# Hybrid encoder step on one core: the outputs of key and value rows issued from ScalarE instead of SyncE

## The chip, the cores and the metric

The kernel runs on one core of one Trainium2 chip. The time is that of the device for one execution, in microseconds (us), and the median of several runs counts. The profile is a recording of one further execution. Its engines are PE (TensorE; PEld is the load of its weights, beside PE), DVE (VectorE), ACT (ScalarE), POOL (GpSimd) and SP (SyncE), which here does nothing but issue transfers (DMAs) and wait. SPq is SP's time in issuing.

## The reference

One layer of an encoder is computed for 1024 prompt rows and 64 sample rows (1088 in all, width 1024), the samples with 512 cached rows before them. Cut to what matters here:

```python
u = rms_norm(h)
z = split_cols(u @ W_in)           # one projection: columns of A, B and C
A = rwkv7_mixer(z['a_*'])          # delta rule with a matrix state, 8 heads
B = fox_attention(b_q, b_k, b_v)   # 8 heads of 64, with a forget gate
C = dsa_attention(c_q, c_k, c_v)   # indexer, top-k of keys, 2 key/value heads
h = h + concat[A*silu(g_A), B*silu(g_B), C*silu(g_C)] @ W_out
# returned beside y: p_b_k, p_b_v, p_c_k, p_c_v (1024 rows each)
#                and s_b_k, s_b_v, s_c_k, s_c_v (64 rows each)
```

So every key and value row is an output as well as an operand of the attention.

## The kernel before, in words

The columns of `W_in` are loaded in blocks of 128 (`load_w`: the block `wraw` is loaded from SP at L130, ACT, POOL split it into three parts `wh`, `wl`, `wb`), and `proj` (L154) multiplies each by the whole of `u`: these matmuls, named `pproj`, are 1088 in each of three kinds. A block's result is "parked": written to a buffer in device memory, from where the attention loads it later. The blocks are projected by generators which yield after every few matmuls, and which the program pumps between the steps of dependent work (top-k, the RWKV units of A, the first attention), so that PE finds projection work while a chain of small steps runs. The order of instructions on each engine is set before the run by a scheduler, from the program's order and a model of its own; each engine then runs its list strictly in order.

The keys of a block are parked by `park_keys`, the values by `park_values`; there are four blocks of two heads for B (`b_k0` to `b_k3`, `b_v0` to `b_v3`) and one for C (`c_k0`, `c_v0`). Both call `rows_out`, ten calls in all. It turns the block (columns by rows) with PE in nine squares, ACT copies these in three steps from PSUM to a tile `rows` of 128 x 9 x 128 (L730), and two DMAs write it to the outputs: L731 the 1024 prompt rows (512 KB), L732 the 64 sample rows (32 KB). In `park_values` the tile is then split into high and low halves by ACT (L771) and POOL (L774), for each of the two heads (`vs` for the new rows, `vcs` for the cached ones), and written to `b_v..` (L775).

Three things tie other work to these two DMAs:

- `rows`, `vs`, `vcs`, `kT`, `kh`, `zg` and others are all tiles of one ring, tag "z", of `NZ=4` buffers. In one call of `park_values` six are taken: `vT`, `rows`, `vs`, `vcs`, `vs`, `vcs`. The sixth, the second `vcs`, gets the buffer of `rows`, so ACT's cast into it (L771) has to wait until both DMAs have read `rows` and landed.
- Every DMA of the kernel is issued from SP, in one order: loads of the attention's operands (`fetch`, L865: `K`, `KL`, `Q`, `QS`, `VS`; gates `sg`, L1117), of weights (L130), stores of parked data. A DMA whose operand isn't there holds those behind it.
- Completions are counted on eight semaphores in turn (DMAHW0 to DMAHW7), over the issues of all engines: each DMA waits until the DMA eight issues earlier has landed.

The attention of B (FoX) runs from about 741 us on: per step, PE computes scores (`ps_sc`, L974 and L975), DVE adds and takes the maximum (L917), ACT the exponential (L921), PE turns the result (`ps_atp`, L107), ACT and DVE split it (`hl`, L943, L944), PE multiplies with the values (`ps_pv`, L1005). That of C follows, and the output projection (L1726) is pumped into it from about 1043 us.

Of the kernel before, what the change touches and what calls it, by code (L numbers as in the profile page):

```python
# [24 lines left out]
P = 128  # L25
# [60 lines left out]
class K:  # L86
# [632 lines left out]
    def rows_out(self, xT, out_p, out_s):  # L719

        nc = self.nc
        row = self.z("rows").rearrange("p (a d) -> p a d", d=P)
        for g in range(3):
            ps = self.tp()
            nb = 4 if g < 2 else 1
            r = P if g < 2 else 64
            for j in range(nb):
                i = 4 * g + j
                self.turn(ps[:r, j * P:(j + 1) * P], xT[:, i * P:i * P + r])
            nc.scalar.copy(row[:r, 4 * g:4 * g + nb, :], ps[:r, :nb * P].rearrange("p (a d) -> p a d", a=nb))  # L730
        nc.sync.dma_start(out=out_p.rearrange("(a p) d -> p a d", p=P), in_=row[:, 0:8, :])  # L731
        nc.sync.dma_start(out=out_s, in_=row[:64, 8, :])  # L732
        return row

    def park_keys(self, col, name, cache, out_p, out_s):
# [1210 lines left out]
```

## Time and profile before

| | before |
|---|---|
| runs | 1293.16, 1289.9, 1292.87 us |
| median | 1292.87 us |
| profiled execution, time | 1289.49 us |
| its span on the core | 1286.6 us |
| PE busy | 1230.5 us (96%) |
| ACT busy | 780.3 us (61%) |
| DVE busy | 843.0 us (66%) |
| POOL busy | 671.7 us (52%) |
| mean granted clock of PE | 0.991 |

The span is from the first to the last instruction of the core. The execution's own time is 2.9 us above it. PE is busy nearly all the time, so what counts is where it isn't: the profile gives each engine's busy time in any stretch, what ended each idle time, and the share of its full speed that PE's clock was granted there.

### The profile page before, as it was taken

The page shows a single profiled execution, that of the slowest core. Times are in us where ns is not written, and L with a number is a line of the kernel's source. Part 1 is how long each engine was busy: PE and PEld are TensorE (multiplying, and loading weights), DVE is VectorE, ACT ScalarE, POOL GpSimd, SP SyncE. Part 2 cuts the span into 40 slices and gives each one's busy share as a digit, 9 for nine tenths or more (in the row PEclk, how much of TensorE's full clock was granted, in tenths as well). Part 3 has the DMA queues.
Part 4 walks back from the last instruction along what each step waited for, and adds up shares of the span by engine and source line. Part 5 has one row for each costly group of instructions (what it writes and reads, how often), then busy time and mean ns, then how long its engine had stood idle before and what let it go on. Part 6 is the DMA issues. An engine that isn't in the chain of part 4 may idle for free.

```text
span 1286.6 us, 29362 instructions
## 1 busy us (share of the span) xinstructions
PE 1230.5 (96%) x10563; PEld 941.8 (73%) x10563; DVE 843.0 (66%) x2487; ACT 780.3 (61%) x1762; POOL 671.7 (52%) x973
## 2 busy tenths in 40 slices
PE   7999999999999999988999989999999889999997
PEld 5777777777777777666777767888887756777764
DVE  7468458888887787998564136556665588666642
ACT  7345357788877888544344456676664587655531
POOL 6333444545545655646454555576666477444311
PEclk9999999999999999989999999999999999999999
DMA  8332421232332443325225389676756476534323
GB/s 231 108 104 68 138 85 52 68 100 71 90 96 73 125 132 105 116 83 170 90 73 162 115 233 268 191 217 201 200 155 183 130 217 171 146 104 114 87 82 95
DMA packets 171699, 168.77 MB, mean 131 GB/s; under 512 B 38641, under 2 KB 146209, under 8 KB 171426
## 3 DMA queue, kind: packets, MB, share of 16 engines
q1 hardware_dynamic: 171554, 166.91, 44.7%
q8 instruction: 83, 1.36, 0.4%
q14 instruction: 62, 0.51, 0.1%
HBM read 106.18 MB, written 62.25 MB: 131 GB/s over the span
## 4 chain that ended last, share of the span: by engine, by line
PE 78%; DVE 9%; DMA 6%; ACT 3%; issue 2%; SPq 1%; POOL 0%; DVEq 0%; POOLq 0%; ACTq 0%
PE pproj L154 37%; PE pproj L1726 7%; PE ps_pv L1005 5%; PE ps_atp L107 4%; PE ps_tp L1726 4%; PE ps_sc L974 2%; PE ps_sc L975 2%; PE ps_gb L1500 2%; PE ps_tp L107 1%; PE ps_gb L1507 1%; ACT junka L613 1%; PE ps_gc L1610 1%; PE ps_gc L1612 1%; PE ps_gc L1601 1%; PE ps_ga L107 1%
## 5 line engine op out<-in xcount | busy, mean ns | idle before, releaser
L154 PE MATMUL pproj<-uH,wh 128*128 128x384 f32 (+4 forms) x1088 | 491.4, 452 | 0.0
L154 PE MATMUL pproj<-uH,wl 128*128 128x384 f32 (+4 forms) x1088 | 361.6, 332 | 0.0
L154 PE MATMUL pproj<-uL,wb 128*128 128x384 bf16 (+4 forms) x1088 | 356.9, 328 | 0.8 <-DVE shift L818 0.5
L154 PEld LDWEIGHTS pproj<-uH,wh 128*128 128x128 f32 (+1 forms) x1088 | 215.8, 198 | 4.8 <-issue 0.7
L154 PEld LDWEIGHTS pproj<-uH,wl 128*128 128x128 f32 (+1 forms) x1088 | 206.5, 190 | 2.0
L154 PEld LDWEIGHTS <-wb 128*128 128x128 bf16 (+1 forms) x1088 | 105.8, 97 | 116.5 <-issue 80.5
L613 ACT ACTIVATE junka<-score,tk_tau 128x1024 f16<-128x1024 f32 (+4 forms) x160 | 149.5, 934 | 33.1 <-DVE junk L607 22.1
L926 POOL TENSOR_SCALAR S<-S,mx 128x128 f32<-128x128 f32 (+8 forms) x136 | 105.6, 780 | 84.1 <-DVE mx L925 62.6
L140 POOL TENSOR_TENSOR wl<-wraw,wh 128x256 fp32r<-128x256 f32 (+1 forms) x184 | 137.8, 780 | 5.8 <-ACT wh L137 4.8
L943 ACT CAST hl<-ps_atp 128x512 fp32r<-128x512 f32 (+3 forms) x184 | 93.6, 515 | 76.8 <-PE ps_atp L107 67.1
L944 DVE TENSOR_TENSOR hl<-ps_atp,hl 128x512 fp32r<-128x512 f32 (+3 forms) x184 | 109.7, 600 | 45.1 <-ACT hl L943 43.4
L921 ACT ACTIVATE S<-S,mx 128x128 f32<-128x128 f32 (+8 forms) x136 | 105.8, 778 | 39.6 <-DVE mx L917 36.1
L142 POOL TENSOR_SCALAR wb<-wraw 128x512 bf16<-128x512 f32 (+1 forms) x92 | 62.9, 701 | 114.3 <-PE pproj L154 66.9
L1005 PE MATMUL ps_pv<-hl,VS 128*128 128x256 f32 (+3 forms) x640 | 111.9, 286 | 7.6 <-ACT hl L943 3.4
L1005 PEld LDWEIGHTS ps_pv<-hl,VS 128*128 128x128 f32 (+1 forms) x640 | 88.7, 173 | 20.7 <-DVE hl L944 4.7
L107 PE MATMUL ps_atp<-ident,S 128*128 128x128 f32 x616 | 101.7, 276 | 1.1 <-DVE hl L944 0.6
L1171 POOL TENSOR_TENSOR cb<-nm,T 128x256 f32<-128x256 bf16 (+2 forms) x80 | 54.3, 685 | 54.5 <-DVE mx L917 52.7
L107 PEld LDWEIGHTS ps_atp<-ident,S 128*128 128x128 f32 x616 | 74.8, 141 | 7.8 <-issue 1.0
L137 ACT CAST wh<-wraw 128x1024 fp32r<-128x1024 f32 (+1 forms) x46 | 47.7, 1037 | 35.9 <-PE pproj L154 35.4
L1726 PE MATMUL pproj<-oh,gh 128*128 128x512 f32 x144 | 67.4, 490 | 0.8 <-ACT oh L1705 0.5
L1726 PE MATMUL pproj<-ol,gb 128*128 128x512 bf16 (+1 forms) x144 | 52.4, 386 | 0.9 <-DVE ol L1706 0.9
L1598 DVE COPY UV<-ps_gd 64x64 f32<-64x64 f32 x136 | 29.9, 220 | 28.7 <-PE ps_gd L1593 26.5
(387 smaller groups left out, 2845.2 us busy)
## 6 DMA issues: line engine op xcount, KB each, us to landing
wraw<-in_w_in_dram SPq DMA_DIRECT2D x45, 512.0 KB
oraw<-in_w_out_dram SPq DMA_DIRECT2D x12, 512.0 KB
out_dram<-rows SPq DMA_DIRECT2D x10, 512.0 KB
x<-in_x_prompt_dram SPq DMA_DIRECT2D x8, 512.0 KB
wt<-a_wa SPq DMA_DIRECT2D x16, 256.0 KB
b_v<-vs SPq DMA_DIRECT2D x8, 512.0 KB
VS<-b_v SPq DMA_DIRECT2D x8, 512.0 KB
d_y<-y SPq DMA_DIRECT2D x64, 64.0 KB
```

The lines of the kernel that those rows point to most:

```text
L107: self.nc.tensor.transpose(out, x, self.ident[:n, :n])
L140: nc.gpsimd.tensor_tensor(l[:, k:k + 2, :n], raw[:, k:k + 2, :n], h[:, k:k + 2, :n], op=OP.subtract)
L142: nc.gpsimd.tensor_scalar(b[:, k:k + 4, :n], raw[:, k:k + 4, :n], 1.0, 0.0, op0=OP.mult, op1=OP.add)
L154: self.nc.tensor.matmul(ps[:n, :nt], a[:, k, :n], b[:, k, t0:t0 + nt], start=(k == 0 and i == 0), stop=(k == KD - 1 and i == 2))
L613: nc.scalar.activation(junk[:, :sc.shape[1]], sc, AF.Sign, bias=tf[:, j:j + 1], accum_out=cnt[:, j:j + 1])
L921: nc.scalar.activation(S[:, :kn], S[:, :kn], AF.Exp, bias=mx[:, nm - 1:nm], scale=-1.0, accum_out=mx[:, 6:7])
L926: nc.gpsimd.tensor_scalar(S[:, :kn], S[:, :kn], mx[:, 7:8], 0.5, op0=OP.mult, op1=OP.mult)
L943: nc.scalar.copy(ph[:kr, a:b], ps[:kr, a:b])
L944: nc.vector.tensor_tensor(pl[:kr, a:b], ps[:kr, a:b], ph[:kr, a:b], op=OP.subtract)
L1005: nc.tensor.matmul(pv[0:m, q0:256], VS[:, kb, 0:m], hl[:, x, o:o + w], start=kb == 0 and x == 0, stop=at[-1][0] == last and n == 3)
L1171: nc.gpsimd.tensor_tensor(o, x, y, op=OP.add)
L1726: nc.tensor.matmul(ps[hf][:n, :], parts[m // 4][q][:, m % 4, :n], self.wo[m][q // 2][:, hf * 512:hf * 512 + 512], start=m == 0 and q == 0, ...
```

## The change

Both output DMAs of `rows_out` are issued by ACT (`nc.scalar`) instead of SP (`nc.sync`). ACT has written the rows. What is copied, to where, and the ring of buffers stay as they are.

```diff
             nc.scalar.copy(row[:r, 4 * g:4 * g + nb, :], ps[:r, :nb * P].rearrange("p (a d) -> p a d", a=nb))
-        nc.sync.dma_start(out=out_p.rearrange("(a p) d -> p a d", p=P), in_=row[:, 0:8, :])
-        nc.sync.dma_start(out=out_s, in_=row[:64, 8, :])
+
+        nc.scalar.dma_start(out=out_p.rearrange("(a p) d -> p a d", p=P), in_=row[:, 0:8, :])
+        nc.scalar.dma_start(out=out_s, in_=row[:64, 8, :])
         return row
```

Lines below it are one higher in the changed kernel (L731 becomes L732, L865 becomes L866). Twenty issues go from SP's list (804 rows before, 784 now) to ACT's. The scheduler sets the order of the other instructions anew as well: the lists are alike up to about 422 us, then differ in pieces, on every engine.

The first place is `b_v3`, the last block of values of B. On SP, before, the two issues stand behind the loads for the first two heads and for the sample queries (the last of these is the gate `sg` at L1117). In brackets is what an instruction waits for.

```order
L865 DMA QS_12081<-b_q0h 64x64 [waits DMAHW4_49]
L865 DMA QS_12082<-b_q0h 64x64 [waits DMAHW5_49,Pool_49]
L865 DMA QS_12082<-b_q0l 64x64 [waits DMAHW6_49]
L865 DMA QS_12082<-b_q0h 64x64 [waits DMAHW7_49]
L1117 DMA sg<-b_g_9844 128x1024 [waits DMAHW0_49]
L731 DMA out_dram<-rows 128x8x128 [waits DMAHW1_49]
L732 DMA out_dram<-rows 64x128 [waits DMAHW2_49]
L865 DMA K<-b_k0h 64x576 [waits DMAHW3_49,PE_49]
```

Now the loads of `K` follow directly on `sg` there. On ACT, in the changed kernel, the same two issues stand among the copies and casts of the rows (L730, L772) and the exponentials (L922):

```order
L922 ACTIVATE S,mx<-S,mx 128x128 [waits DVE_49]
L732 DMA out_dram<-rows 128x8x128 [waits DMAHW2_49,Activation_49]
L922 ACTIVATE S,mx<-S,mx 128x256 [waits DVE_49]
L772 CAST vs<-rows 128x8x64 [waits DMAHW7_49,Pool_49]
L772 CAST vcs<-kc 128x4x64 [waits DMAHW1_49]
L730 COPY rows<-ps_tp 64x128 [waits PE_49]
L772 CAST vs<-rows 128x8x64
L922 ACTIVATE S,mx<-S,mx 128x384 [waits DVE_49]
L733 DMA out_dram<-rows 64x128 [waits DMAHW6_49,Activation_49]
```

The cast into the buffer of `rows` comes seven rows later on ACT, behind the exponential of 640 keys; before the change it stood behind that of 1024 keys, three exponentials later:

```order
L922 ACTIVATE S,mx<-S,mx 128x640 [waits DVE_49]
L954 COPY tmp<-ps_pv 64x256 [waits PE_49]
L772 CAST vcs<-kc 128x4x64 [waits DMAHW6_49,DMAHW2_49,Pool_49]
L922 ACTIVATE S,mx<-S,mx 128x768 [waits DVE_49]
L944 CAST hl<-ps_atp 128x512 [waits PE_49]
```

So the cast waits for the two DMAs (their counters are DMAHW2 and DMAHW6) and for POOL, and it does so earlier in ACT's list than before.

The second place is SP about 25 us later, ahead of the first load of the next block's keys, `K<-b_k1h`. Before:

```order
L746 DMA c_k0h<-kcs 128x512 [waits DMAHW2_49,Activation_49]
L747 DMA c_k0l<-kcs 128x512 [waits DMAHW3_49,DVE_49]
L130 DMA wraw<-in_w_in_dram 128x8x128 [waits DMAHW4_49,Pool_49]
L865 DMA K<-b_k1h 64x1024 [waits DMAHW5_49,PE_49]
L865 DMA K<-b_k1h 64x1024 [waits DMAHW6_49]
```

In the changed kernel:

```order
L763 DMA kc<-in_cache_c_v_dram 128x4x128 [waits DMAHW0_49,PE_49]
L797 DMA b_g_12354<-zg 128x1088 [waits DMAHW1_49,DVE_49]
L747 DMA c_k0h<-kcs 128x512 [waits DMAHW2_49,Activation_49]
L866 DMA K<-b_k1h 64x1024 [waits DMAHW3_49,PE_49]
L866 DMA K<-b_k1h 64x1024 [waits DMAHW4_49]
```

The store `c_k0l` and the load of a block of weights, which stood ahead of it, now come behind it.

The third place is PE before the first matmul of the output projection. Between a run of six transposes (the same in both) and that matmul, the list before held 40 matmuls of the attention of C, whose last rows were:

```order
L975 MATMUL ps_sc<-KL,cQ 128x384
L1005 MATMUL ps_pv<-hl,VS 128x128
L1005 MATMUL ps_pv<-hl,VS 64x128
L1005 MATMUL ps_pv<-hl,VS 64x256
L1005 MATMUL ps_pv<-hl,VS 128x256
L107 MATMUL ps_atp<-ident,S 128x128 x3
L1726 MATMUL pproj<-oh_15961,gh 128x512 x2
```

In the changed kernel it holds 59, and ends so:

```order
L107 MATMUL ps_atp<-ident,S 128x128 x3
L975 MATMUL ps_sc<-K,cQ 128x512
L976 MATMUL ps_sc<-KL,cQ 128x512
L1006 MATMUL ps_pv<-hl,VS 128x128
L975 MATMUL ps_sc<-K,cQ 128x384
L976 MATMUL ps_sc<-KL,cQ 128x384
L1006 MATMUL ps_pv<-hl,VS 64x128
L1006 MATMUL ps_pv<-hl,VS 64x256
L1006 MATMUL ps_pv<-hl,VS 128x256
L107 MATMUL ps_atp<-ident,S 128x128 x3
L1727 MATMUL pproj<-oh_15961,gh 128x512 x2
```

Two pairs of scores, eight products with the values and seven transposes have moved ahead of the output projection's first matmul.

## Rows read from the trace of the kernel before

**Rows 1.** The page: busy us of each engine, share of the span, instructions.

```profile
PE 1230.5 (96%) x10563; PEld 941.8 (73%) x10563; DVE 843.0 (66%) x2487; ACT 780.3 (61%) x1762; POOL 671.7 (52%) x973
```

**Rows 2.** Windows: us busy of 20 by engine, PE's clock, DMA share, GB/s.

```profile
540.00:560.00 20.00, 14.82 (x147) 11.12 (x147) 18.65 (x40) 7.15 (x15) 13.01 (x17) 0.86 0.36 120
740.00:760.00 20.00, 18.99 (x119) 14.80 (x118) 5.42 (x23) 9.62 (x25) 13.64 (x25) 1.00 0.97 248
760.00:780.00 20.00, 15.45 (x92) 12.12 (x91) 12.17 (x39) 12.17 (x30) 7.42 (x11) 0.91 0.87 246
1020.00:1040.00 20.00, 13.11 (x79) 10.62 (x77) 15.57 (x57) 14.31 (x37) 12.13 (x21) 0.91 0.74 214
```

**Rows 3.** Everything on the tile rows: ns min/median/max, and who waited.

```profile
L730 ACT COPY rows<-ps_tp x30: 243/580/593, 418.7 to 845.0; 128x512 f32<-128x512 f32 x20, 64x128 f32<-64x128 f32 x10
...
L731 SPq DMA_DIRECT2D out_dram<-rows x10: 378/389/533, 421.4 to 840.9; - x10
L732 SPq DMA_DIRECT2D out_dram<-rows x10: 476/490/583, 423.6 to 846.0; - x10
...
  ACT vcs L771: 4.7, 2
```

**Rows 4.** Timeline of ACT, 744 to 776 us: start, duration, operation, idle before.

```profile
753.90 0.26 ACT L730 COPY rows<-ps_tp 64x128 f32<-64x128 f32 x1 [0.24 <-PE ps_tp L107]
...
758.64 0.37 ACT L953 COPY tmp<-ps_pv 64x256 f32<-64x256 f32 x1
...
766.34 0.19 ACT L921 ACTIVATION_READ_ACCUMULATOR S<-S,mx 128x1 f32 x1
770.17 0.40 ACT L771 CAST vcs<-kc 128x256 fp32r<-128x256 f32 x1 [3.65 <-DMA out_dram<-rows]
```

**Rows 5.** Timeline of SP's issues, 744 to 804 us.

```profile
764.28 0.43 SPq L731 DMA_DIRECT2D out_dram<-rows  x1
764.76 0.58 SPq L732 DMA_DIRECT2D out_dram<-rows  x1
...
788.67 0.44 SPq L747 DMA_DIRECT2D c_k0l<-kcs  x1
789.20 0.47 SPq L130 DMA_DIRECT2D wraw<-in_w_in_dram  x1
790.81 1.09 SPq L865 DMA_DIRECT2D K<-b_k1h  x2
```

**Rows 6.** The chain that ended last, 744 to 776 us: start, duration, what.

```profile
746.35 7.55 DMA sg<-b_g
...
753.91 8.56 DMA VS<-b_v
...
764.76 5.32 DMA out_dram<-rows
```

**Rows 7.** Timeline of PE, single rows at 771 and 797 us.

```profile
771.39 0.33 PE L1005 MATMUL ps_pv<-hl,VS 128*128 128x128 f32 x1 [3.41 <-ACT hl L943]
...
797.77 0.30 PE L974 MATMUL ps_sc<-K,Q 128*128 128x128 f32 x1 [0.52 <-DMA K<-b_k1h]
```

**Rows 8.** Windows of 2 us behind the stop (columns as in Rows 2).

```profile
768.00:770.00 2.00, 0.00 (x0) 0.00 (x0) 0.00 (x0) 0.00 (x0) 0.00 (x0) 1.00 1.14 355
770.00:772.00 2.00, 0.34 (x2) 0.21 (x2) 0.79 (x3) 1.83 (x7) 1.35 (x2) 1.00 1.06 230
772.00:774.00 2.00, 1.91 (x11) 1.35 (x11) 0.77 (x4) 1.53 (x5) 2.00 (x5) 0.72 1.06 233
774.00:776.00 2.00, 1.86 (x8) 1.56 (x9) 1.18 (x2) 0.46 (x1) 0.53 (x1) 0.50 1.01 227
776.00:778.00 2.00, 1.55 (x11) 1.27 (x10) 0.89 (x3) 1.23 (x3) 0.00 (x0) 0.93 0.99 370
```

**Rows 9.** Windows of 10 and 20 us around the output projection's start (columns as before).

```profile
1034.00:1044.00 10.00, 6.57 (x42) 5.12 (x42) 8.87 (x27) 8.16 (x19) 5.74 (x9) 1.00 0.71 203
1040.00:1060.00 20.00, 18.92 (x100) 11.69 (x101) 18.34 (x53) 17.16 (x38) 15.40 (x16) 1.00 0.69 195
```

## The prediction

> **What bounds the kernel.** I read the page first: PE is busy 96% of the span [rows 1], so a change can only win where PE stands, or lose by making it stand. The windows show where that is [rows 2]: most lose little, but 540 to 560 us has 14.82 of 20 us, 760 to 780 has 15.45 and 1020 to 1040 has 13.11. Of these only the second is near one of the ten places where rows are written out.
>
> I then asked for all that touches the tile `rows`, and for who waits on it [rows 3]. The issues take SP 389 and 490 ns in the median, ten times each, from 421 to 846 us. Only one wait on them is of any size: ACT's cast `vcs`, 4.7 us in two places. One of the two is the stop in the second stretch: ACT ends an exponential's sum at 766.34 + 0.19 = 766.53 us and stands for 3.65 us, until 770.17, for the output of `rows` to land [rows 4]; the other has the rest, 1.05 us. PE's product with the values then waits for ACT's `hl`, 3.41 us [rows 7], and the windows around it show every engine at nothing from 768 to 770 us [rows 8].
>
> Why it lands so late: the last copy of these rows starts on ACT at 753.90 us [rows 4], but SP issues the two outputs only at 764.28 and 764.76 [rows 5]. SP was not waiting for the rows. The chain shows what it waited for: the landing of `sg` (7.55 us) and of `VS` (8.56 us), loads of the attention that hold one of the eight completion counters each [rows 6]. From the last issue, the landing took 5.32 us [rows 6].
>
> **The change, part by part.**
>
> *The stop at 766 us, gain.* On ACT the first issue comes after the second copy of rows, at about 752 us, the second after the third copy, at about 755.5 us: some 12 and 9 us earlier. The counters they need were last held, by the new lists, by the first load of `Q`, four issues ahead of `sg`, and by `sg` itself, which landed at 746.35 + 7.55 = 753.90 [rows 6], so ACT should not stand there. Landing: at best 5.32 us after the issue, as the same output did under less load, at worst 8.56 us, as a load of 512 KB did in this very stretch, where the DMA share is 0.97 [rows 2, 6]. For the first output this gives 757 to 760.9 us, for the second (32 KB, behind it) 761 to 764. The cast now comes earlier in ACT's list, behind `tmp` that ends at 758.64 + 0.37 = 759.0 us [rows 4]. So it stands from nothing to 5 us there; PE was busy 18.99 of 20 us from 740 to 760 [rows 2], with projection work among its steps, which hides a stand of ACT of a microsecond or so; I take it at nothing, and its far end is rival 2. If the stop at 766 us is gone, PE gains its 3.41 us and the clock that it lost: the three windows behind it were granted 0.72, 0.50 and 0.93 of full speed [rows 8], a loss of (0.28 + 0.50 + 0.07) x 2 = 1.70 us. Together 5.11 us, the upper bound. The lower bound is 0.
>
> *How much of it stays.* PE's next wait for SP is at 797.77 us, 0.52 us for `K<-b_k1h` [rows 7], and from 764 us on the DMAs are at a share of 0.99 to 1.14 [rows 8]. SP comes free for this load at 789.20 + 0.47 = 789.67 us and issues it at 790.81, when PE has released the buffer [rows 5]. In the new order the rows' issues (0.43 + 0.58 us), the store of `c_k0l` (0.44) and a load of weights (0.47) no longer stand before it: SP can be free 1.92 us earlier, some 0.1 us of gaps more, at about 787.6 us. So the load can follow PE by 790.81 - 787.6 = 3.2 us, and what PE gains beyond that it stands for again at this load. I take 3.2 us as the gain.
>
> *ACT's new work, loss.* The issues cost ACT 10 x (0.389 + 0.490) = 8.8 us if they take as long there as on SP [rows 3]; the trace has no DMA issued by ACT. ACT is at 61% [rows 1], and in most of the stretch PE has projection work between ACT's steps. Lower bound 0; upper bound 8.8, if all of it lay on the path. Nearer is the first, since only `b_v3` lies among dependent steps, where two issues take 0.88 us; I take 0.5 us.
>
> *The other nine places.* The one other wait on `rows` is ACT's 1.05 us, and no row has PE standing behind it; what it could give is 0 to 1.05 us, and I take 0.
>
> *The new order, loss or gain.* At the output projection's start, 19 more matmuls of the attention come ahead of the first of the projection. In 1034 to 1044 us, where the last of the 40 ran, PE was busy 6.57 of 10 us [rows 9]. 19 matmuls at a mean of 6.57/42 = 0.156 us are 3.0 us of work and at that share another 1.5 us of standing. Later fewer such steps are left between projection work, but PE has only 1.08 us of standing in 1040 to 1060 to give back [rows 9]. Bounds: -1.1 (that is given back and the rest costs nothing) and +3.0 (an estimate: twice 1.5, since single large ones take 0.30 to 0.33 us [rows 7] and not 0.156); I take 1.3, near the middle. In 540 to 560 us DVE is busy 18.65 of 20 [rows 2] and its list there, the end of the top-k, is shuffled: bounds -2 and +2 (an estimate: two fifths of the 5.18 us that PE stands there), taken as 0.
>
> **The sum.** -3.2 + 0.5 + 1.3 + 0 = -1.4 us against the profiled execution's 1289.49 us: 1288.1 us. The median shown is 1292.87 us, 3.4 us above it, and one of the three runs (1289.9) is like it; against the median the forecast is 1291.5 us, -0.1%. About 0.3%, 3.9 us, is what a measurement of this kernel can tell from no change, so this is a forecast of no change that can be told.
>
> The Trainium skill, in DMA: Bandwidth & Descriptors (Issuing engines are not separate DMA queues), says that DMAs issued by several engines run on the same 16 DMA engines, and that issuing from more than one saves only the time of issue, usually small beside the DMA itself. By that the sum would hold the issue time alone and be within 1 us of nothing; the trace bears it out for nine of the ten places, but at `b_v3` the rows stood 10 us for their issue [rows 4, 5], so there an earlier issue is an earlier start.
>
> **The rivals.**
>
> 1. *The whole stop goes and all stays gone* (faster). If the loads from 787 us on keep ahead of PE, as the DMA share may allow once 544 KB have moved from a full stretch into an earlier one, and the order costs nothing: 1292.87 - 5.1 = 1287.8. For it: PE waited only 0.52 us for any load here [rows 7]. With the top-k's -2 it would be 1285.8.
>
> 2. *The stop only moves* (no change). The outputs land by 764 us, not by 759, and ACT's cast, now earlier in its list, stands about as long as before, 3 to 5 us; PE then stands 3.4 us and loses the clock some 7 us sooner. With the taken costs: 1292.87 + 1.8 = 1294.7. For it: the stretch is at a DMA share of 0.97 [rows 2] and loads took 7.55 and 8.56 us [rows 6]. Against it: PE has projection work until 760 us.
>
> 3. *ACT stands at its issues* (slower). A DMA issued by ACT waits in ACT's list for the counter's last holder to land, and what follows are exponentials and `hl`, for which PE waits at once. If one of the holders is a load that SP itself issued late, ACT stands for its 5.32 to 8.56 us. As 3.65 us on ACT cost PE 3.41 us and 1.70 us of clock [rows 4, 7, 8], one such stand of 7 us costs some 6.8 + 1.7 = 8.5 us, against which stands the gain of 3.2: 1292.87 + 8.5 - 3.2 + 1.8 = 1299.9. It decides from a stand of about 5 us. For it: the last four issues (`c_k0`, `c_v0`) wait for counters that loads of `QS` and `K` of the attention held. Against it: by SP's list these were issued many instructions earlier.
>
> **How the numbers follow.** My forecast, some gain at 766 us partly given back, 0.45. Rival 1, 0.22; rival 2, 0.17; rival 3, 0.16. The predicted time is 1291.5 us. From 1286 (rival 1 with part of the top-k's bound) to 1297 us (rival 3 with a stand of 4 to 5 us, 1292.87 + 4.1) all but some 2 in 10 is held. The forecast's own range is 1288.5 to 1294.5 us. Faster by over 0.3%: rival 1 and a tenth of the forecast's share, 0.27. Slower by over 0.3%: rival 3 and the upper end of rival 2, 0.21. Within: 0.52.
>
> **What would show it.** Right, if the outputs of `b_v3` are issued on ACT near 752 and 755 us, ACT's cast waits under 1 us, PE has no stop of over 1 us between 760 and 772 us with the clock at 1.00 there, and a wait for `K<-b_k1h` of 0.5 to 2 us comes near 795 us. The output projection would start with PE at under 14 of 20 us, as before. Wrong, if ACT is seen waiting 3 us or more for `rows` or at a DMA, if the wait in front of `K<-b_k1h` takes back all of the gain, or if the order alone (540 to 600 us, 1020 to 1060 us) moves PE's idle time by more than 3 us.

## Result, and the profile after

| | before | after |
|---|---|---|
| median of 6 runs | 1291.41 us (1288.54 to 1293.91) | 1297.95 us (1296.8 to 1300.3) |
| ratio, 95% interval | 1 | 1.0053 (1.0035 to 1.0071) |
| profiled execution, time | 1289.49 us | 1298.25 us |
| its span | 1286.6 us | 1296.5 us |
| mean granted clock of PE | 0.991 | 0.987 |

The change made the kernel slower by 0.53%. The forecast was 1291.5 us, no change; the result lies above the top of its range, 1297 us.

The page of the kernel after, busy time and DMA queues (number of packets, MB, share of the 16 engines):

```profile
PE 1236.5 (95%) x10563; PEld 945.6 (73%) x10563; DVE 839.2 (65%) x2487; ACT 779.2 (60%) x1762; POOL 670.7 (52%) x973
q1 hardware_dynamic: 160354, 161.33, 42.4%
q10 hardware_dynamic: 11200, 5.57, 1.6%
```

No engine has more work; PE's 6.0 us beside [rows 1] are the same instructions, in part at a lower clock. ACT's transfers have a queue of their own, q10. The rest of the 9.9 us of span is standing, and the next views say where.

Windows after, columns as in [rows 2]; three of its four stretches and the one that follows the third place:

```profile
540.00:560.00 20.00, 16.40 (x178) 12.33 (x177) 18.69 (x41) 7.66 (x18) 15.36 (x18) 0.83 0.40 134
760.00:780.00 20.00, 15.63 (x97) 13.12 (x96) 12.10 (x41) 11.95 (x30) 11.17 (x18) 0.91 0.71 185
1020.00:1040.00 20.00, 16.19 (x97) 13.80 (x97) 13.30 (x52) 12.48 (x34) 11.61 (x23) 0.83 0.66 200
1040.00:1060.00 20.00, 16.46 (x82) 11.73 (x80) 16.39 (x53) 16.58 (x39) 11.71 (x17) 0.83 0.69 192
```

Read against [rows 2, 9], these mislead: 760 to 780 us seems unchanged and 540 to 560 better, but the work has shifted, so a stretch no longer holds the same work. What can be compared is the start of the same matmul (the n-th of the projection's L154, or of the attention's L1005) in two traces. By that the kernel after is late against before by:

| at (us, before) | 421.6 | 705.6 | 746.8 | 900 | 1016 | end |
|---|---|---|---|---|---|---|
| after | 1.3 | 4.7 | 4.7 | 4.5 | 6.6 | 9.9 |

So the stretch of `b_v3`, from which the forecast took its gain and its chief risks, gave and took nothing (-0.1 us from 747 to 900). The losses lie before it (3.3 us from 422 to 706) and behind it. The first 1.3 us lie where the lists are still alike and come in most executions laid beside this one trace of before: so far one execution scatters.

Most of the 2.1 us from 900 to 1016 us fell at one place, from 997 to 1005 us after, where the granted clock was 0.76 and then 0.82 in windows of 4 us: for part of them PE ran at the lower of its two levels, 1.2 in place of 2.4 GHz. Before had 1.00 in the same work (992 to 1000 us), as has every other trace here, though PE stood as much at its start (busy 2.72 of 4 us before, 2.62 after). With one trace of this kernel, whether that is scatter or its own isn't known.

**At `b_v3`.** The timeline of ACT after (start, duration, operation, idle before and what ended it):

```profile
756.25 0.38 ACTq L732 DMA_DIRECT2D out_dram<-rows  x1
...
758.24 0.26 ACT L730 COPY rows<-ps_tp 64x128 f32<-64x128 f32 x1 [0.15 <-PE ps_tp L107]
...
758.62 0.47 ACTq L733 DMA_DIRECT2D out_dram<-rows  x1
...
763.38 0.37 ACT L954 COPY tmp<-ps_pv 64x256 f32<-64x256 f32 x1
767.98 0.40 ACT L772 CAST vcs<-kc 128x256 fp32r<-128x256 f32 x1 [4.23 <-DMA out_dram<-rows]
```

The issues come as soon as the rows are written, as forecast: less the 4.7 us by which this trace is late, at 751.6 and 753.9 us. But the cast, now behind `tmp`, stands 4.23 us where it stood 3.65 [rows 4]. The chain has what it waited for:

```profile
758.62 9.26 DMA out_dram<-rows
```

The landing took 9.26 us from the last issue, above the forecast's worst case of 8.56 [rows 6]. The DMA view, from 756 to 761 us and then from 761 to 768 us, shows that it began late:

```profile
q1 hardware_dynamic: 405, 1.38, 105.7%
```

```profile
q1 hardware_dynamic: 494, 1.20, 57.9%
q10 hardware_dynamic: 1120, 0.56, 31.9%
```

The output was issued at 756.25 us, yet its queue q10 has no packet before 761: for some 5 us only loads that SP had issued on q1 moved. The waits of PE after, 755 to 815 us (total, times, longest):

```profile
PE ps_pv L1006 <- ACT hl L944: 3.6, 1, 3.6
PE pproj L154 <- DVE zg L796: 1.4, 1, 1.4
```

PE's 3.41 us [rows 7] have become 3.6. The stop has moved, from 768 us in before to 766 in after; with the lateness of 4.7 us taken off, it comes some 6 us sooner in the work.

**A new stand, on SP.** SP's timeline and, below it, its waits in the same stretch:

```profile
761.72 0.33 SPq L1104 DMA_DIRECT2D sgs<-b_g  x1
767.77 0.45 SPq L866 DMA_DIRECT2D QS<-b_q0h  x1
```

```profile
SPq L866 <- DMA out_dram<-rows: 5.7, 1, 5.7
```

SP has nothing to do with `rows` any more and yet stands 5.7 us for their landing. The order of the changed kernel says why. SP's issues from the load of `KL` at 752.46 us on, with the counters that they wait for:

```
L866 DMA KL<-b_k0l 64x1024 [waits DMAHW1_49]
L866 DMA KL<-d_ck 2x1024 [waits DMAHW3_49]
L866 DMA Q<-b_q0h 64x1024 [waits DMAHW4_49]
L866 DMA Q<-b_q0l 64x1024 [waits DMAHW5_49]
L866 DMA Q_1_12078<-b_q0h 64x1024 [waits DMAHW7_49]
L866 DMA VS<-b_v_7535 128x1024 [waits DMAHW0_49]
L1104 DMA sgs<-b_g_8002 128x64 [waits DMAHW1_49]
L866 DMA QS_12081<-b_q0h 64x64 [waits DMAHW2_49,Pool_49]
```

DMAHW2 and DMAHW6 are missing where their turn would be: ACT's two outputs have them. The next on DMAHW2 is SP's `QS`, which waits for the 512 KB output to land, and all loads stand behind it. Windows of 2 us of the same work, first before, then after (columns as in [rows 2]; the last but one is the DMA share):

```profile
761.00:763.00 2.00, 2.00 (x10) 1.17 (x9) 1.94 (x8) 1.64 (x3) 0.91 (x1) 1.00 0.39 95
763.00:765.00 2.00, 2.00 (x18) 1.77 (x16) 1.94 (x7) 1.35 (x5) 1.01 (x1) 1.00 0.33 29
765.00:767.00 2.00, 1.90 (x16) 1.81 (x15) 2.00 (x8) 1.52 (x3) 0.73 (x1) 1.00 0.66 174
```

```profile
766.00:768.00 2.00, 0.33 (x2) 0.00 (x0) 0.00 (x0) 0.02 (x1) 0.00 (x0) 1.00 0.47 164
768.00:770.00 2.00, 0.02 (x1) 0.02 (x1) 0.65 (x2) 1.98 (x5) 1.53 (x3) 1.00 0.07 15
770.00:772.00 2.00, 2.00 (x9) 1.65 (x10) 2.00 (x8) 1.34 (x3) 0.77 (x1) 0.59 0.09 20
772.00:774.00 2.00, 2.00 (x14) 2.00 (x12) 1.21 (x5) 0.87 (x3) 1.02 (x1) 0.56 0.35 56
```

Before had a hole here too, at shares of 0.39, 0.33 and 0.66, some 3.2 us of the transfers' time. After it is deeper and longer, from 0.47 over 0.07 and 0.09 to 0.35, some 6.0 us: about 2.8 us more are lost in the busiest stretch (an estimate from these windows).

**Ahead of it, 422 to 706 us.** Two of PE's waits that grew. Before:

```profile
PE ps_gc L1601 <- DVE UV L1598: 0.9, 3, 0.4
PE ps_gb L1507 <- DVE T L1543: 0.7, 2, 0.5
```

After:

```profile
PE ps_gb L1508 <- DVE T L1544: 2.7, 3, 1.7
PE ps_gc L1602 <- DVE UV L1599: 2.0, 2, 1.9
```

No output of rows is in these. The timeline of DVE shows the new order at work. Before, the RWKV unit's `T` runs ahead of the top-k's first step (L666):

```profile
549.83 0.41 DVE L1543 TENSOR_TENSOR T<-T,ps_gb 128x256 f16<-128x256 f16 x1
...
550.68 1.07 DVE L666 TENSOR_SCALAR_CACHE_REDUCE eq<-sg 128x896 f16<-128x896 f16 x1
```

After, it stands behind that and behind the top-k's long scan:

```profile
552.62 2.66 DVE L674 TENSOR_TENSOR_SCAN cum<-one,eq 128x896 f16<-128x896 f32 x1
...
555.36 0.42 DVE L1544 TENSOR_TENSOR T<-T,ps_gb 128x256 f16<-128x256 f16 x1
```

PE waits for `T` at 555.83 us, 1.67 us after its last matmul had ended.

These two waits show how the order works, but they aren't where the time went. Two traces can be laid side by side wherever PE has done the same instructions in both. Between two such points around both waits (527.0 to 563.5 us before, 529.1 to 566.1 after) the kernel after takes only 0.5 us longer: PE stands 6.1 us in place of 5.4, since its stands for `QR`, for `BK` and at an issue, 4.1 us before, are gone. Of the 3.3 us, 1.3 arise from 422 to 438 us and 1.5 from 643 to 661 (times of before); the rest, of either sign, comes to 0.5. Both steps are the same in every trace with this order (the kernels e2, e6 and e12 of the next section: 1.3 and 1.5 us in each). In the second, PE after has a stand that before hasn't:

```profile
PE ps_tp L107 <- DVE BA L1449: 0.8, 1, 0.8
```

What makes up the other 0.7 us there wasn't found.

### The profile page after: what moved, and what is told of

Read it like the earlier page. It is cut to its first block, busy times and chain, and to the rows that moved or that the text cites. A ratio compares the mean times of both kernels' runs of the same rounds, so it can differ in the third digit from the quotient of the medians.

```text
span 1296.5 us, 29342 instructions
## 1 busy us (share of the span) xinstructions
PE 1236.5 (95%) x10563; PEld 945.6 (73%) x10563; DVE 839.2 (65%) x2487; ACT 779.2 (60%) x1762; POOL 670.7 (52%) x973
## 4 chain that ended last, share of the span: by engine, by line
PE 78%; DVE 9%; DMA 5%; ACT 4%; issue 2%; POOL 1%; SPq 1%; DVEq 0%; POOLq 0%; ACTq 0%
PE pproj L154 36%; PE pproj L1727 7%; PE ps_pv L1006 5%; PE ps_atp L107 5%; PE ps_tp L1727 4%; PE ps_sc L975 2%; PE ps_sc L976 2%; PE ps_gb L1501 2%; ACT junka L613 1%; PE ps_tp L107 1%; PE ps_gc L1611 1%; PE ps_gb L1508 1%; DVE junk L607 1%; PE ps_gc L1602 1%; PE ps_gc L1613 1%
## 5 line engine op out<-in xcount | busy, mean ns | idle before, releaser
L154 PE MATMUL pproj<-uH,wh 128*128 128x384 f32 (+4 forms) x1088 | 491.7, 452 | 0.0
L154 PE MATMUL pproj<-uH,wl 128*128 128x384 f32 (+4 forms) x1088 | 361.1, 332 | 0.0
L154 PE MATMUL pproj<-uL,wb 128*128 128x384 bf16 (+4 forms) x1088 | 357.1, 328 | 2.3 <-DVE zg L796 1.7
L154 PEld LDWEIGHTS pproj<-uH,wh 128*128 128x128 f32 (+1 forms) x1088 | 216.1, 199 | 6.4 <-issue 2.4
L154 PEld LDWEIGHTS pproj<-uH,wl 128*128 128x128 f32 (+1 forms) x1088 | 206.6, 190 | 2.0
L154 PEld LDWEIGHTS <-wb 128*128 128x128 bf16 (+1 forms) x1088 | 105.9, 97 | 116.0 <-issue 80.7
L922 ACT ACTIVATE S<-S,mx 128x128 f32<-128x128 f32 (+8 forms) x136 | 105.8, 778 | 45.5 <-DVE mx L918 42.1
L1172 POOL TENSOR_TENSOR cb<-nm,T 128x256 f32<-128x256 bf16 (+2 forms) x80 | 50.2, 635 | 61.2 <-DVE mx L918 45.5
L1539 DVE TENSOR_TENSOR Y<-ps_gb,con 128x256 f16<-128x256 f32 x85 | 35.5, 418 | 19.5 <-PE ps_gb L1508 18.8
```

The source lines that it names most:

```text
L154: self.nc.tensor.matmul(ps[:n, :nt], a[:, k, :n], b[:, k, t0:t0 + nt], start=(k == 0 and i == 0), stop=(k == KD - 1 and i == 2))
L922: nc.scalar.activation(S[:, :kn], S[:, :kn], AF.Exp, bias=mx[:, nm - 1:nm], scale=-1.0, accum_out=mx[:, 6:7])
L1172: nc.gpsimd.tensor_tensor(o, x, y, op=OP.add)
```

## Experiments

The theory after the result had two parts: the new order of DVE and PE costs most of the loss with no issue moved; and at `b_v3` the gain is eaten by waits that the change itself makes (ACT's cast, SP's shared counter). The rival was that the moved issues cost the time themselves, at each of the ten places. The ratios below are to runs of the kernel before on the same chip, with 95% intervals.

**Parts of the change.** `rows_out` is told the block's name, and only some blocks issue from ACT; the scheduler is free. The edit of the kernel before in e1 (blocks of C):

```diff
-        nc.sync.dma_start(out=out_p.rearrange("(a p) d -> p a d", p=P), in_=row[:, 0:8, :])
-        nc.sync.dma_start(out=out_s, in_=row[:64, 8, :])
+        (nc.scalar if name[0] == "c" else nc.sync).dma_start(out=out_p.rearrange("(a p) d -> p a d", p=P), in_=row[:, 0:8, :])
+        (nc.scalar if name[0] == "c" else nc.sync).dma_start(out=out_s, in_=row[:64, 8, :])
```

In e2 the condition picks `b_k0` to `b_k2` and `b_v0` to `b_v2`, in e3 `b_v3`.

The blocks of C alone (e1): 

> Only the outputs of the rows of c_k and c_v (4 of the 20 issues, near 845 us) go to ACT; the other 16 stay on SP. Up to about 770 us all lists of instructions are those of before; from about 1020 us PE's list is that of the changed kernel. Theory A (the order): most of the changed kernel's loss from 970 us on, 5.3 us between the two traces (4.5 to 9.9 us of delay), comes from the new order of the attention of C and the output projection, so this kernel loses 3 to 5 us (ratio 1.0025 to 1.004), and 1020 to 1060 us shows the same stops as the changed kernel. Theory B (the issues themselves cost): PE has no idle time at 820 to 960 us, so the four issues cost nothing and the ratio is 1.000 +- 0.001.

Measured: 1293.26 us, ratio 1.0015 (0.9999 to 1.0031). At the output projection its list of PE is that of after, with 59 matmuls ahead of the projection's first; by the ratio that costs 0.0015 x 1291.2 = 1.9 us, not clear of nothing.

The first three pairs of B (e2): 

> Only the outputs of b_k0 to b_k2 and b_v0 to b_v2 (12 issues, 421 to about 690 us) go to ACT. PE's list up to about 640 us is that of the changed kernel, from there to about 1010 us that of before, later a third one. Theory A (the order): the loss by 700 us is that of the changed kernel, about 3.3 us, where the lists differ (540 to 640 us), though no issue of ACT stands there for its counter. Theory B: the same loss, but as stands of ACT or SP at these issues and at what waits for their counters. Both expect a ratio of 1.002 to 1.004 plus or minus what the late order brings; which of them holds is read from the waits at the places where delay grows.

Measured: 1295.9 us, 1.0038 (1.0019 to 1.0056). In its trace it loses 3.3 us from 422 to 706 us, like after. It lost another 5.1 us from 747 to 900 us, where its order and issues are those of before; so one trace can differ by several us there, by scatter or because it comes 4.6 us late to that place, which this trace doesn't tell apart.

`b_v3` alone (e3): 

> Only the two outputs of b_v3 go to ACT, the place on which the prediction rested. PE's list is that of before up to about 730 us, that of the changed kernel up to 840 us, and a third one from about 1020 us. Theory A: ACT's stop moves from 766 us to about 759 us with 3.5 to 4.5 us, as in the changed kernel, PE's time from 740 to 850 us changes by less than 1 us, and the end moves only by the late order (0 to +4 us). Rival, the prediction's reasoning: the stop shrinks and 2 to 3 us are gained by 850 us.

Measured: 1292.47 us, 1.0017 (1.0003 to 1.003). The one place with a stop to remove gains nothing either.

**Without the wait, first try.** In before, with all issues on SP, the second `vcs` is made in place in `kc`, so that nothing waits for the buffer of `rows` (e4).

```diff
-                    s = self.z("vcs", F32R).rearrange("p (a d) -> p a d", d=P)
+                    s = kc.bitcast(F32R) if e else self.z("vcs", F32R).rearrange("p (a d) -> p a d", d=P)
```

> The kernel before, all outputs of rows from SP, but the second vcs is built in place in the tile kc, so no cast waits for the outputs of rows. What the wait itself is worth: by the prediction's sum the stop at 766 us goes with its 3.4 us and 1.7 us of clock, of which 3 to 5 us stay by 850 us; by the rival view, that the loads behind set PE's pace, under 1 us stays. The order of the lists changes from 470 us on in this kernel too, so by theory A the end may move by 3 to 5 us either way for that alone: the reading is the delay between 740 and 850 us.

Measured: 1303.31 us, 1.0099 (1.0077 to 1.012). The stop's worth can't be read from it: the scheduler rearranged everything from 470 us on, and from 422 to 706 us, ahead of the place, it lost 14.5 us. This is a warning of how large the effect of the order is, and so the next kernels hold it.

**Holding the order.** A call at the program's end ties each instruction of an engine to the one that a table lists ahead of it, in place of the scheduler's choice. It adds no wait: in the kernel with `b_v3` on POOL (e9, below) the lists of PE, DVE, ACT and POOL, and their waits for one another, are those of before but for the two issues.

```diff
             program(ctx, tc, I, O)
+            pin(nc, tc)
...
+        for d in part.split(","):
+            at += int(d)
+            i = traced[at]
+            if last is not None:
+                tc.add_manual_dep(i, last.name, info, reason="pinned order")
+            last = i
```

All twenty issues on ACT, everything else in before's order (e5): 

> The changed kernel (all 20 issues on ACT) with every engine's other instructions held in the order of the kernel before, by edges that order issue alone. Theory A (the order costs, not the issue): the loss goes, ratio at most 1.000; and as ACT's cast then stands behind the exponential of 1024 keys again, near 767 us, when the rows have landed, the stop there goes as the prediction had it, with 2 to 5 us (0.996 to 0.9985). Theory B (the issues, their counters or the second queue cost): the loss stays, 1.004 to 1.006, with stands of ACT or SP at 421 to 700 us.

All on SP, in after's order (e6): 

> The kernel before (all 20 issues on SP) with every engine's other instructions held in the order of the changed kernel. Theory A: the loss is there without any issue on ACT, ratio 1.004 to 1.007, the delay growing at the same places (540 to 700 us, 970 to 1050 us), and ACT's cast, now behind the exponential of 640 keys, waits longer for the rows than in the changed kernel (some 8 to 11 us, from 759 to 770 us), which adds up to 5 us. Theory B: ratio 1.000 +- 0.001.

| | before's order | after's order |
|---|---|---|
| issued from SP | 1 | 1.011 (1.0095 to 1.0125) |
| issued from ACT | 1.0029 (1.0017 to 1.0042) | 1.0053 (1.0035 to 1.0071) |

So the two parts don't add. With before's order the issues on ACT cost 0.3%; with after's order they win 0.6%, because there the cast stands early in ACT's list and would wait long for SP's late issue. The waits of ACT and PE in the kernel with SP and after's order, 755 to 815 us:

```profile
PE ps_pv L1005 <- ACT hl L943: 9.4, 1, 9.4
ACT vcs L771 <- DMA out_dram<-rows: 10.0, 1, 10.0
```

In the kernel with ACT and before's order the stop at 766 us is gone: PE is 2.8 us ahead of before at 771 us. Then it loses more. (The profiled execution took 1297.18 us, 3.2 above its kernel's median, so this trace shows more loss than is usual.) Its waits of PE and SP, 755 to 815 us:

```profile
PE pproj L154 <- DVE zg L796: 5.1, 1, 5.1
PE ps_sc L975 <- DMA K<-b_k1h: 1.8, 1, 1.8
SPq L866 <- DMA out_dram<-rows: 5.6, 1, 5.6
```

And its windows of 4 us:

```profile
764.00:768.00 4.00, 3.90 (x32) 3.53 (x30) 3.85 (x15) 3.40 (x9) 2.10 (x3) 1.00 0.08 18
...
776.00:780.00 4.00, 1.07 (x10) 0.90 (x9) 0.00 (x0) 0.00 (x0) 0.47 (x1) 1.00 1.02 274
```

PE runs through 764 to 768 us at 3.90 of 4 us while the DMAs stand at 0.08; ten us later, from 776 to 780, it is busy 1.07 of 4 us. ACT's `zg` needs the ring buffer of a `vs`, whose store SP could issue only behind its stand and the loads queued there, and the projection waits for `zg`.

The in-place cast in before's order, on SP (e7) and on ACT (e8): 

> The kernel before (issues on SP) in its own order, held, with the second vcs built in place in the tile kc, so no cast waits for the outputs of rows: the wait alone, without a new order. By the prediction's sum 3.2 us are gained by 850 us (0.9975), at most 5.1 (0.996); if the loads behind set PE's pace, under 1 us (1.000).

> Both: all 20 issues on ACT and the second vcs in place, in the held order of the kernel before. If the issue on ACT is worth something beyond the wait that it shortens, this is faster than the kernel without the wait; if it costs, slower. Theory A expects both within 0.1% of each other (0.996 to 0.998); theory B expects this one slower by 0.3% or more.

Measured: 1296.46 us, 1.0046 (1.0034 to 1.0058), and 1298.86 us, 1.0062 (1.0049 to 1.0075). PE gained 3.6 us from 747 to 771 us in the first, but the edit has a price of its own, since the next load of `kc` now waits for the store out of it:

```profile
PE ps_tp L107 <- DMA kc<-in_cache_c_k_dram: 3.1, 1, 3.1
SPq L739 <- DMA b_v<-kc: 2.8, 1, 2.8
```

So these two don't measure what the stop is worth; they show only that its removal is at once followed by a wait for the next load.

**Without the shared counter.** Only `b_v3`'s two outputs leave SP, once to POOL (e9) and once to ACT (e10), in before's order for all else. POOL's two DMAs are counted on two counters that none of SP's has. The edit of e9 (e10 has `nc.scalar` in its place, e11 `nc.gpsimd` for all ten):

```diff
-        nc.sync.dma_start(out=out_p.rearrange("(a p) d -> p a d", p=P), in_=row[:, 0:8, :])
-        nc.sync.dma_start(out=out_s, in_=row[:64, 8, :])
+        (nc.gpsimd if name == "b_v3" else nc.sync).dma_start(out=out_p.rearrange("(a p) d -> p a d", p=P), in_=row[:, 0:8, :])
+        (nc.gpsimd if name == "b_v3" else nc.sync).dma_start(out=out_s, in_=row[:64, 8, :])
```

> Order of the kernel before, held; only the two outputs of b_v3 are moved, and to POOL, whose DMAs are counted on other completion counters than the eight that SP and ACT share. Theory C (what costs with the issue on ACT is SP's stand: its next load on the same counter waits until ACT's output has landed, and everything behind it on SP comes later): SP does not stand there, the DMAs have no hole near 765 us, ACT's stop at 766 us is gone, and of its 3.4 us at least 2 remain at 850 us: ratio 0.997 to 0.999. Rival D (the loads behind set PE's pace whatever the rows do): PE stands the same 3 to 5 us at 780 us for zg or kc, delay at 850 us is 0 or above, ratio 1.000 to 1.004.

> The same with ACT in place of POOL: only the outputs of b_v3 on ACT, order of the kernel before held. Theory C: SP stands 5 to 6 us at the load of QS behind them, PE gains 3.5 us at 766 us and loses 6 to 9 by 810 us: ratio 1.002 to 1.004, as with all 20 issues on ACT in this order (1.0029), since the other 18 cost nothing. If the other 18 carry that loss, this one is at 1.000 +- 0.001.

Measured: on POOL 1288.17 us, 0.9993 (0.9979 to 1.0008); on ACT 1292.38 us, 1.0018 (1.0005 to 1.0032). Against each other, ACT is 3.6 us slower in the mean (1.8 to 5.3; an estimate from the 12 runs of each). SP's `QS` waits for DMAHW0 in the first, which an old load held, and for DMAHW2 in the second, which ACT's output holds. The waits in the second, on ACT:

```profile
PE pproj L154 <- DVE zg L795: 5.5, 1, 5.5
ACT zg L794 <- DMA b_v<-vs: 6.6, 1, 6.6
SPq L865 <- DMA out_dram<-rows: 5.5, 1, 5.5
```

In the first, on POOL, SP has no such wait, but PE is stopped all the same:

```profile
PE ps_sc L974 <- DMA K<-b_k1h: 2.4, 1, 2.4
PE pproj L154 <- DVE zg L795: 1.6, 1, 1.6
```

PE went from 1.1 us late at 747 us to 1.9 us ahead at 771 and was 2.2 us late at 806: the 3.0 us won were all given back, at the load of `K` and at `zg`. This execution took 1292.07 us, though, 3.9 above its kernel's median; by the ratio the kernel gains 0.9 us (from 2.7 gained to 1.0 lost), so in others some of it may stay. The ratio also shows that holding the order costs nothing that can be measured.

All ten on POOL (e11): 

> All 20 outputs on POOL, order of the kernel before held. Theory C: as the one with b_v3 alone, 0.997 to 0.999, since the other places have no stop to lose. If POOL's issues are dear (its casts vs and wl stand behind them), slower than that one by more than 0.2%.

Measured: 1297.5 us, 1.006 (1.0041 to 1.008). Its trace falls back by 3.3 us near 590 us (`b_v1`) and 3.2 us near 690 us (`b_v2`). At the first, a scan of the top-k on DVE (L674) took 4.17 us where before had 1.24, and PE waited 2.7 us for `za` behind it; why the scan took so long the trace doesn't say. At the second, POOL's second issue came only at 692.31 us, behind its products `vs`; ACT's `zg` waited for that output to land, and PE 1.8 us for `zg`. So on POOL the issues have a price of their own, as the expectation allowed.

**The order by pieces.** After's order only up to 700 us, all issues on SP (e12): 

> All issues on SP; up to about 700 us every engine's other instructions are held in the order of the changed kernel, behind that in the order of the kernel before. If the new order of the top-k and the RWKV units costs what the traces show for it (delay at 700 us 3.3 us above that at 420 us in the changed kernel, 4.2 us with the issues on SP, 0.6 us with ACT in the old order), the ratio is 1.0025 to 1.0035, and the delay grows between 430 and 680 us and nowhere else by more than 1.5 us. If that was chance of single executions: 1.000 +- 0.001.

Measured: 1296.46 us against 1291.61, 1.0027 (1.0014 to 1.0041). By the ratio that is 0.0027 x 1291.61 = 3.5 us for the order alone. Its waits of PE from 470 to 700 us:

```profile
PE ps_gb L1507 <- DVE T L1543: 3.4, 3, 2.4
PE ps_gc L1601 <- DVE UV L1598: 2.0, 2, 1.8
```

They are like those of after, with no issue moved, and so is the stand for `BA` (0.8 us).

All issues on ACT, after's order only from 700 to 870 us, before's elsewhere (e13): 

> All issues on ACT; the order of the kernel before is held up to 700 us and from 870 us on, that of the changed kernel between: the b_v3 stretch as in the changed kernel. There the changed kernel's delay went from 4.65 to 4.51 us, so if that holds and the rest of its loss is the order elsewhere, this one is at 1.000 to 1.0015, and faster than ACT with the old order throughout (1.0029).

Measured: 1290.46 us, 0.9989 (0.998 to 0.9998). This is the change without the two pieces of order that cost: 0.11% faster than before, with an interval that ends just under 1, less than the 0.3% that counts as told here. Against the change itself, 1.0053 (1.0035 to 1.0071), the intervals lie far apart: with all twenty issues on ACT, putting before's order back in those two pieces removes the whole loss. At `b_v3` it has both stands of after:

```profile
PE ps_pv L1006 <- ACT hl L944: 3.5, 1, 3.5
SPq L866 <- DMA out_dram<-rows: 5.5, 1, 5.5
```

Its lateness against before goes from 1.4 us at 747 to 0.8 at 900 us.

The lateness of all these traces in the two pieces that differ by the order:

| | 422 to 706 us | 1016 us to the end |
|---|---|---|
| after's order there | after +3.3, e2 +3.3, e6 +4.2, e12 +6.4 | after +3.3, e1 +3.7, e6 +1.9 |
| before's order there | e1, e3, e5, e9, e10, e13: -0.9 to +0.6 | e5, e7 to e13: +0.2 to +2.4, mean 1.1 |

Three kernels with before's order in the first piece are left out of it, since their own edits cost there: e7 +2.1 and e8 +4.4 (PE waits 2.6 us for `kc` near 697 us in e7, and as long in e8), e11 +7.6 (above). In the second piece e2 and e3 have orders of their own. Ahead of the first matmul of the projection they have 18 and 2 matmuls fewer than before, where after has 19 more, and they lose 0.7 and 4.1 us: the number of them isn't what costs. The second piece is the weaker one. The granted clock from 1020 to 1060 us was 0.83 in after and e1 and 0.96 in before, e10 and e13, but also 0.83 in e5, e7 and e12, which have before's order there and lose 1.7 to 2.4 us; so part of its loss is a clock that falls in either order.

## Why the prediction was wrong, step by step

- **The new order, loss or gain.** This is the larger of two steps that failed. The forecast saw the shuffled list of DVE at 540 to 560 us and took it as 0, with bounds of -2 and +2. The new order ahead of 700 us costs 0.27%, 3.5 us (1.8 to 5.3), when it alone is changed, and the four traces that have it lose 3.3 to 6.4 us: beyond the bound. The forecast also priced the wrong place. It compared the lists at three places and looked for the rest where PE stood in before, but of after's 3.3 us only some 0.5 arise there, and 2.8 from 422 to 438 and from 643 to 661 us, in stretches that it did not look at. Which swap in the lists costs them is not shown. At the output projection 1.3 us was taken; the blocks of C alone give 1.9 us by the ratio, and the traces 3.0 - 1.1 = 1.9 us, with a scatter as large: about right.
- **The stop at 766 us, gain.** This is the other step that failed, and rival 2 came in place of it. The forecast had the cast at 759 us, with a stand of nothing to 5 us, of which projection work would hide the first, and took it as nothing. It stood 4.23 us, from 763.75 to 767.98, and PE had run out of projection work by 766. The step's bounds for the landing were too narrow: 9.26 us against at most 8.56, since the new queue's packets started only 5 us after the issue. Together with ACT's new work the forecast had 2.7 us gained; the change with order held elsewhere (e13) gives 0.11%, 1.4 us (0.3 to 2.6).
- **What the forecast didn't name.** It asked whether ACT would wait for the counters of SP's loads, and not whether SP would wait for those of ACT's outputs. The order shown with it had the numbers DMAHW2 and DMAHW6 beside the two outputs; two lists read together would have given `QS` as the next holder. With before's order, where the stop does go, this stand of 5.5 us is what the traces show between 0.9993 and 1.0018; the two kernels differ in the issuing engine and its queue as well, so the stand as the only cause is read, not shown.
- **How much of it stays.** 3.2 us was taken, on the ground that the loads could follow. Even without SP's stand (`b_v3` on POOL) the trace shows 3.0 us won and nothing of it kept: the load of `K<-b_k1h` took 7.39 us from its issue where before had 6.32. By that kernel's ratio at most 2.7 us stay. All six traces in which the stop at 766 us is gone (e5, e7 to e11) are later against before at 900 us than at 747, by 0.5 to 6.2 us. So it looks as if the transfers set the pace in this stretch, and a stop of PE ahead of one is little that can be won back; no run tries this by itself.
- **ACT's new work, loss.** 0.5 us was taken. The issues take 378 and 487 ns in the median on ACT, as on SP, and no wait of PE for them is seen. Rival 3, ACT standing at its issue, wasn't seen: a load that ACT waited for at an issue cost it 0.4 us, once. Its mirror image, SP standing for ACT's output, was.
- **The other nine places** were taken as 0, and the traces that issue them from ACT in before's order (422 to 706 us: e5 +0.6, e13 +0.1 us) agree.

The sum by the ratios: early order +0.27%, late order +0.15%, the change in between -0.11%, together +0.31% of the 0.53% (0.35 to 0.71) measured. The rest is within the intervals of the parts. What is shown is that the two pieces of order together carry the loss (1.0053 with them, 0.9989 without, the issues being the same). How it divides between them is known only as far as these intervals go, and the late piece alone is not clear of nothing.

One of the prediction's own signs of being wrong came: ACT waited more than 3 us for `rows`. The sign that it set for the order looked at PE from 540 to 600 us and from 1020 to 1060 us, away from most of the early loss. Two of its sums are slightly off, and nothing hangs on them: the first output's latest landing is 752 + 8.56 = 760.6 us and not 760.9, and rival 3 gives 1300.0 and not 1299.9.

The Trainium skill's rule that was weighed (DMA: Bandwidth & Descriptors, Issuing engines are not separate DMA queues) would have had the change within 1 us of nothing. The trace agrees that both queues share the 16 DMA engines (57.9% and 31.9% of them from 761 to 768 us); the time came out 6.5 us away from no change, by the order of the lists, of which that rule says nothing.

## What to carry to other kernels

Where a scheduler sets the order, a change of one line is a change of every list: compare the lists of all engines over their whole length, not only where the busiest engine stood before, and hold the order to measure the edit itself. Read the loss between points where the busiest engine has done the same work in both traces: a wait that grew may only have taken the place of another. Where completions are counted on a few counters in turn over several engines, look up who is next on the counter of each moved transfer, since a slow transfer of one engine then stops another engine's loads. And a stop of the busiest engine is worth only what the next load allows: ask, before counting it as gain, when that load can be there.

## What the runs showed of the hardware

- A transfer issued by ACT at 756.25 us moved no packet until 761.08 us, while loads of SP's queue kept the DMAs at a share of 1.06. At the other nine places the first packet came 0.9 to 2.9 us after the issue, and 1.3 to 1.9 us at the three where the DMAs were as full (shares of 0.99 to 1.04 in the 5 us behind the issue, at 725.66, 819.97 and 843.20 us); so a full stretch alone isn't the reason, which stays open. The Trainium skill (DMA: Bandwidth & Descriptors, Queues, rings and completion order) has each DMA engine go round between its queues packet by packet; by that the output, once queued, would have moved at a part of the rate. From 761 us on the trace agrees: both queues move side by side (41 packets of q1 and 170 of q10 from 761 to 762 us). Of the 4.8 us ahead of it, it shows nothing.
- The eight counters in turn are those of SP's and ACT's transfers. The two that POOL issued (e9) were counted on two others.
- One issue takes ACT as long as SP: 373 to 434 ns (median 378) and 474 to 532 ns (487) for the two outputs, beside [rows 3].
